# A diffusion block on one core: fewer VectorE instructions in the mixers and in the first norm

## The chip, the cores and the metric

The kernel runs on 1 core of one Trainium2 chip. The metric is the device time of one execution in microseconds (us); a lower one is better. Engines are named as in the profile: PE is TensorE's matmuls (PEld its weight loads), DVE is VectorE, ACT is ScalarE, POOL is GpSimd, and SP is SyncE, whose queue starts nearly all DMAs. Each engine works its own list of instructions strictly in order; a list is fixed when the kernel is built. Semaphores hold an instruction back until what it needs is done.

## The reference

One layer (DEPTH 1) on a latent stream of 1024 tokens and a context stream of 256, both 1024 wide. One input projection is split among four mixers (mLSTM in both directions, a spatial-gating MLP called SGU, a convolution module, a state-space scan S5 in both directions), their outputs are joined and projected, and two norms stand around a SwiGLU feed-forward network.

```python
h = x * (1.0 + sc1) + sh1
hc = xc * (1.0 + sc1c) + sh1c
z = h @ w_in_l
...
y_a, yc_a = mlstm_mixer(z[..., :OFF_B], zc_a, ...)        # two directions, summed, then normed per head
y_b = sgu_mixer(z[..., OFF_B:OFF_C], ...)                 # u * (w_s @ layer_norm(gelu(v)) + b_s)
y_c = conv_mixer(z[..., OFF_C:OFF_D], ...)                # silu(layer_norm(conv31(a * sigmoid(g))))
y_d, yc_d = s5_mixer(z[..., OFF_D:], zc_d, ...)           # complex scan, both directions
y = jnp.concatenate([y_a, y_b, y_c, y_d], axis=-1) @ w_out[l]
x = layer_norm(ALPHA * x + g1 * y, ln1_w[l], ln1_b[l])
x = layer_norm(ALPHA * x + g2 * swiglu(x * (1.0 + sc2) + sh2, w_ffn_in[l], w_ffn_out[l]), ln2_w[l], ln2_b[l])
```

## The kernel before, in words

Everything is fp32. A large product is made of three matmuls on parts: each operand is split into a high and a low part in a 32-bit matmul format (`split2`: ACT casts the high part, DVE subtracts to get the low one, lines L854 and L855), and PE adds hi*hi, hi*lo and lo*hi.

The program is written out mixer by mixer, and a scheduler at build time sorts the instructions into one list for each engine: it takes what it thinks ready, so that projections (`projT` L884, `projK` L893) fill PE between the small matmuls of the mixers. Tiles come from pools with a fixed number of buffers; a tile that takes over a buffer waits until the last reader of the tile before it is done.

The stages, by the time at which they run in the profile:

- up to 60 us: modulation, loads, splitting of the inputs.
- 60 to 220 us: S5. `s5_unit_tables` makes sine and cosine tables (`Es`, `Ec`) for four units; `s5_unit` projects two groups of states into PSUM (`X`, L287), turns them by the tables on DVE (`t1`, `t2`, `s`, L292 to L299), scans (L302), and turns them back (L306 to L310), for both directions `d`. For the reverse direction it reads `X` backwards in two pieces, since context (32 columns) and latent (128) are each reversed. `U`, the input in chunks, goes through DRAM (`zd`).
- 230 to 420 us: mLSTM in 8 chunks (`mlstm_chunk`; `mlstm_norm` for two chunks at a time), the convolution's taps on DVE, then SGU and the convolution's norm. `ln_stats` makes mean and 1/std with bn_stats on DVE and a square root on ACT; `sgu_norm` (L636) and `conv_norm` (L696) normalise on DVE.
- 375 to 496.5 us: `out_proj` for tokens 0 to 511 (half 0), interleaved with the mixers' end, then for half 1. For each of two column halves `c` and four token tiles `t` it adds 24 matmuls of 128x512 into a bank (L1184), DVE multiplies by the gate (L1188) and adds the residual into `XN` (L1189).
- `ln1(half)`: for each of four token tiles bn_stats on DVE (L1195), a square root on ACT (L1147), and on ACT the normalisation of 128x1024 (L1154); then for eight k four transposes on PE (L1204), two evacuations by ACT that apply the next modulation (`hi` L1207, `t_` L1208), and the low part on DVE (L1209). The results are the pages `H2`, which the feed-forward network reads. `page` gives buffers of a pool of 9, `page2` and `page3` those of two others.
- From 498.7 us: the feed-forward network (L884, then L1345 and L1470), and the second norm, which already makes its sums by accumulation (L1491, L1501).

Of the kernel before, what the change touches and what calls it, by code (L numbers as in the profile page):

```python
# [167 lines left out]
NP = 2  # L168


def s5_unit_tables(e, S, u, tp, wp):
# [77 lines left out]

    Ec, Es = (tp.tile([128, 2, NP, 160], F32, name=f"s5E{x}") for x in "cs")  # L250
    for d in range(2):
        f, n = Es[:, d], wp.tile([128, NP, 160], F32, name="s5ta", tag="s5ta")
# [13 lines left out]
        a.activation(Ec[:, d], Ec[:, d], AF.Copy, scale=-2.0, bias=1.0)  # L266
# [7 lines left out]
def s5_unit(e, S, T, u, U, Yg, wp):  # L274
# [4 lines left out]
    for P in range(NP):  # L279
        SS = []  # L280
        for d in range(2):
# [3 lines left out]
            for gi in range(2):  # L285
                for ri in range(2):
                    pe.matmul(X[gi * 64:(gi + 1) * 64, ri, :], lhsT=T.WT[:, P, d, ri, gi * 64:(gi + 1) * 64],  # L287
                              rhs=U(2 * (P0 + P) + gi), start=True, stop=True)
            t1, t2, s = (wp.tile([128, 2, 160], F32, name=f"s5{x}", tag=f"s5{x}") for x in ("r1", "r2", "sc"))
            Ec, Es = T.Ec[:, d, P, None, :], T.Es[:, d, P, None, :]  # L290
            if d == 0:
                v.tensor_tensor(t1, X, bc(Ec, [128, 2, 160]), op=MUL)  # L292
                v.tensor_tensor(t2, X, bc(Es, [128, 2, 160]), op=MUL)
            else:
                for t, E_ in ((t1, Ec), (t2, Es)):
                    v.tensor_tensor(t[:, :, 0:32], X[:, :, 31::-1], bc(E_[:, :, 0:32], [128, 2, 32]), op=MUL)
                    v.tensor_tensor(t[:, :, 32:160], X[:, :, 159:31:-1], bc(E_[:, :, 32:160], [128, 2, 128]), op=MUL)
            v.tensor_tensor(s[:, 0], t1[:, 0], t2[:, 1], op=ADD)
            v.tensor_tensor(s[:, 1], t1[:, 1], t2[:, 0], op=SUB)  # L299
            r8 = bc(S.r8[:, dp:dp + 1], [128, 160])  # L300
# [8 lines left out]
            v.tensor_tensor(o[:, 0], q1[:, 0], q2[:, 1], op=SUB)
            v.tensor_tensor(o[:, 1], q1[:, 1], q2[:, 0], op=ADD)  # L310
            SS.append(SD)
# [210 lines left out]
def mlstm_chunk(e, G, c, qT, kT, vx, hb, wp):  # L522
# [33 lines left out]
    for hh in range(2):  # L556
        for d in range(2):
            wi = G.TW[:, 1, d].rearrange("p (r h c) -> p r h c", r=2, h=2)
            v.tensor_tensor(tmp[:, d, hh * 2:hh * 2 + 2], I[hh][:, 0:260].rearrange("p (r d x) -> p r d x", r=2, d=2)[:, :, d],
                            bc(wi[:, :, hh, step(d):step(d) + 1], [128, 2, 65]), op=MUL)  # L560
    for d in range(2):
# [5 lines left out]
    for d in range(2):
        i = 2 + c if d == 0 else 9 - c
        dn = tmp[:, d, :, 64].rearrange("p (h r) -> p h r", h=2)
        g = G.TW[:, 2, d].rearrange("p (r h c) -> p h r c", r=2, h=2)[:, :, :, i]  # L570
        v.scalar_tensor_tensor(r[:, d], dn, -1.0, dn, op0=MUL, op1=MAX)
        v.tensor_tensor(r[:, d], r[:, d], g, op=MAX)
# [44 lines left out]
def ln_stats(e, srcs, wp, tag, n):  # L617
# [8 lines left out]
    e.nc.scalar.activation(mv[:, :, 1], mv[:, :, 1], AF.Sqrt)
# [57 lines left out]
def conv_norm(e, x, y, q, lnw, lnb, wp):  # L684
# [10 lines left out]
    for i in range(2):  # L695
        v.tensor_scalar(xn[:, i], ps[:, i * 256:(i + 1) * 256], mv[:, i, 0:1], mv[:, i, 1:2], op0=SUB, op1=MUL)  # L696
# [66 lines left out]
def body(tc, A, out):  # L763
# [5 lines left out]
    with st:  # L769
# [369 lines left out]

        lns = cp.tile([128, 8, 14], F32, name="Gk", tag="Gk")  # L1140

        def stats(t):

            st6, mv = lns[:, t, 0:12], lns[:, t, 12:14]
            v.bn_aggr(mv, st6)
            v.tensor_scalar(mv[:, 1:2], mv[:, 1:2], 1e-5, None, op0=ADD)
            a.activation(mv[:, 1:2], mv[:, 1:2], AF.Sqrt)  # L1147
            v.reciprocal(mv[:, 1:2], mv[:, 1:2])
            return mv

        def layer_norm(r, t, dst):
            mv = stats(t)
            v.tensor_scalar(mv[:, 0:1], mv[:, 0:1], mv[:, 1:2], -1.0, op0=MUL, op1=MUL)
            a.activation(dst, r, AF.Identity, scale=mv[:, 1:2], bias=mv[:, 0:1])  # L1154

# [8 lines left out]
        def out_proj(half):  # L1164
# [12 lines left out]
            for c in range(2):  # L1177
                cs_ = slice(c * 512, (c + 1) * 512)
                Ws = {kk: wtile(A["wo"][c, kk], 2, 512, pool_tag=tag) for kk, tag in ((3, None), (1, None), (2, page), (0, page))}
                for t in range(4):  # L1180
# [7 lines left out]
                    v.tensor_tensor(t_, ps, g1[:, cs_], op=MUL)  # L1188
                    v.scalar_tensor_tensor(x_, x_, ALPHA, t_, op0=MUL, op1=ADD)  # L1189

        def ln1(half, new):
            for t in range(half * 4, half * 4 + 4):
                xn = XN[t // 2][:, t % 2]
                for c in range(2):
                    v.bn_stats(lns[:, t, c * 6:c * 6 + 6], xn[:, c * 512:(c + 1) * 512])  # L1195
# [377 lines left out]
```

## Time and profile before

| | us |
|---|---|
| median of 3 runs (lowest to highest) | 1174.7 (1173.6 to 1176.86) |
| the profiled execution | 1174.02 |
| its span, first to last instruction | 1172.2 |
| PE busy | 1133.1 (97%) |
| DVE busy | 930.0 (79%) |
| ACT busy | 445.6 (38%) |

A row of the timeline gives the start, the duration, the engine, the line, the operation and its tiles, how many were merged (x), and in brackets the idle time before it with what ended it. A row of groups gives the count, then the busy time in us and the mean of one in ns, then the idle time before. A row of a window gives its length and each engine's busy time with its number of instructions, then PEclk, the share of the full clock that TensorE was granted. Matmuls are drawn longer than they hold the engine: twelve that start every 0.227 us are drawn at about 0.39 us each, so that PE looks busy through a wait of less than some 0.16 us.

### The profile page before, as it was taken

How to read it: one execution, taken by the hardware profiler on the slowest of the kernel's cores; microseconds unless marked ns; L12 is line 12 of the kernel's file. 1: busy time of each engine (PE TensorE's matmuls, PEld its weight loads, DVE VectorE, ACT ScalarE, POOL GpSimd, SP SyncE). 2: the span in 40 equal slices, each digit the busy share in tenths (PEclk: the TensorE clock that was granted, in tenths of full speed). 3: DMA queues.
4: the chain of work that ended last, by engine and by line, in shares of the span. 5: the costliest groups of instructions: out<-in, count | busy, mean ns of one | idle time of the engine just before them, and what ended most of it. 6: DMA issues, size and time to landing. Idle time of an engine off the chain costs nothing.

```text
span 1172.2 us, 15295 instructions
## 1 busy us (share of the span) xinstructions
PE 1133.1 (97%) x5671; PEld 895.4 (76%) x5671; DVE 930.0 (79%) x1851; ACT 445.6 (38%) x691; POOL 9.6 (1%) x30
## 2 busy tenths in 40 slices
PE   6999999999999999989999999999999999999996
PEld 1487788667888788868887888888887778888884
DVE  6588999978899889879968676777778767766775
ACT  1454444522326433582233332333232336433431
POOL 0010000000000000000000000000000000000000
PEclk9999999999999999999999999999999999999998
DMA  9542111022143346362333545345445679766621
GB/s 359 212 133 89 42 46 57 27 71 70 57 141 109 99 157 212 99 225 73 108 123 112 196 179 180 134 153 192 170 154 202 255 259 349 238 196 220 195 103 72
DMA packets 63147, 177.87 MB, mean 152 GB/s; under 512 B 5537, under 2 KB 9793, under 8 KB 61282
## 3 DMA queue, kind: packets, MB, share of 16 engines
q1 hardware_dynamic: 62658, 175.93, 43.3%
q8 instruction: 44, 0.72, 0.3%
q0 software_dynamic: 272, 0.70, 0.2%
q10 hardware_dynamic: 144, 0.29, 0.1%
q14 instruction: 29, 0.24, 0.1%
HBM read 136.54 MB, written 40.35 MB: 151 GB/s over the span
## 4 chain that ended last, share of the span: by engine, by line
PE 77%; DVE 13%; DMA 4%; issue 4%; ACT 2%; POOL 0%; DVEq 0%; ACTq 0%; POOLq 0%
PE mm L1345 16%; PE mm L884 13%; PE a L1345 8%; PE mm L1470 6%; PE mm L1184 4%; PE b L1345 4%; PE b L884 4%; PE a L1470 3%; PE b L1470 3%; PE mm L893 3%; PE c L1470 2%; PE b L564 1%; DVE whl L855 1%; DVE pg L855 1%; DMA raw<-in_w_dram 1%
## 5 line engine op out<-in xcount | busy, mean ns | idle before, releaser
L854 ACT CAST whl<-raw 128x512 fp32r<-128x512 f32 (+1 forms) x198 | 120.3, 622 | 283.2 <-PE mm L884 69.6
L884 PE MATMUL mm<-pg,whl 128*128 128x512 f32 x816 | 217.7, 406 | 1.4 <-ACT pg L1207 1.2
L1345 PE MATMUL mm<-pg,whl 128*128 128x512 f32 x864 | 205.9, 390 | 0.4 <-DVE whl L855 0.3
L1345 PEld LDWEIGHTS mm<-pg,whl 128*128 128x128 f32 x864 | 161.9, 188 | 35.6 <-issue 0.8
L884 PEld LDWEIGHTS mm<-pg,whl 128*128 128x128 f32 x816 | 147.7, 190 | 38.8 <-issue 6.1
L855 DVE TENSOR_TENSOR whl<-raw,whl 128x512 fp32r<-128x512 f32 (+1 forms) x198 | 133.6, 689 | 46.3 <-ACT whl L854 44.7
L1345 PE MATMUL a<-pg,whl 128*128 128x512 f32 x432 | 104.7, 390 | 3.6 <-ACT whl L854 3.6
L1345 PEld LDWEIGHTS a<-pg,whl 128*128 128x128 f32 x432 | 80.7, 188 | 21.3 <-ACT whl L854 4.8
L855 DVE TENSOR_TENSOR pg<-raw,pg 128x1024 fp32r<-128x1024 f32 (+1 forms) x52 | 59.6, 1149 | 20.8 <-ACT pg L854 20.7
L855 DVE TENSOR_TENSOR pg<-whl,pg 128x1024 fp32r<-128x1024 f32 (+1 forms) x42 | 47.4, 1133 | 31.9 <-ACT pg L854 31.6
L854 ACT CAST pg<-raw 128x1024 fp32r<-128x1024 f32 (+1 forms) x52 | 51.5, 992 | 48.9 <-DMA raw<-in_w_dram 18.0
L854 ACT CAST pg<-whl 128x1024 fp32r<-128x1024 f32 (+1 forms) x42 | 41.1, 980 | 65.9 <-PE c L1470 25.2
L893 PE MATMUL mm<-whl,pg 128*128 128x256 f32 (+1 forms) x448 | 63.1, 288 | 0.0
L893 PEld LDWEIGHTS mm<-whl,pg 128*128 128x128 f32 x448 | 58.1, 190 | 1.5 <-issue 1.1
L1345 PE MATMUL b<-pg,whl 128*128 128x512 f32 x216 | 51.9, 389 | 0.0
L1184 PE MATMUL mm<-pg 128*128 128x512 f32 x192 | 50.8, 409 | 0.0
L1184 PE MATMUL mm<-whl,pg 128*128 128x512 f32 x192 | 50.2, 398 | 0.3 <-DVE pg L1172 0.3
L1470 PE MATMUL mm<-pg,pg 128*128 128x512 f32 x171 | 48.0, 389 | 0.0
L1470 PE MATMUL a<-pg,pg 128*128 128x512 f32 x162 | 47.2, 390 | 0.2 <-DVE hs L1484 0.2
L1470 PE MATMUL b<-pg,pg 128*128 128x512 f32 x162 | 47.1, 389 | 0.0
L1345 PEld LDWEIGHTS b<-pg,whl 128*128 128x128 f32 x216 | 40.5, 188 | 8.4
L1184 PEld LDWEIGHTS mm<-pg 128*128 128x128 f32 x192 | 37.4, 198 | 8.6 <-DVE pg L855 0.7
(468 smaller groups left out, 1838.2 us busy)
## 6 DMA issues: line engine op xcount, KB each, us to landing
raw<-in_w_dram SPq DMA_DIRECT2D x59, 512.0 KB
gd<-pg SPq DMA_DIRECT2D x22, 1024.0 KB
whl<-gd SPq DMA_DIRECT2D x35, 512.0 KB
pg<-in_w2k_dram SPq DMA_DIRECT2D x11, 1024.0 KB
td<-pg SPq DMA_DIRECT2D x11, 1024.0 KB
raw<-td SPq DMA_DIRECT2D x20, 512.0 KB
pg<-in_wm_dram SPq DMA_DIRECT2D x16, 512.0 KB
raw<-in_wo_dram SPq DMA_DIRECT2D x16, 512.0 KB
```

The costliest lines, as they stand in the source:

```text
L564: pe.matmul(ps[:, x * 65:(x + 1) * 65], lhsT=D[d][:, x], rhs=vx[:, h, :], start=True, stop=True)
L854: a.copy(hi, r)
L855: v.tensor_tensor(lo, r, hi.bitcast(F32), op=SUB)
L884: pe.matmul(ps[h], lhsT=W(wi, k), rhs=rhs(hi, h, k), **f)
L893: pe.matmul(ps, lhsT=lhs(hi, k), rhs=Ws[k // 4](wi, k % 4), start=(k == 0 and n == 0), stop=(k == 7 and n == 2))
L1184: pe.matmul(ps, lhsT=Yr(hi, half, k)[:, t * 128:(t + 1) * 128], rhs=Ws[k // 2](wi, k % 2), start=(i + n == 0), stop=(i == 7 and n == 2))
L1345: pe.matmul(ps, lhsT=W[:, wi, k, :], rhs=B[b][hi][:, k], start=(first and k + n == 0), stop=(k == 3 and n == 2), skip_group_check=True)
L1470: pe.matmul(ps[t], lhsT=Ag[:, hi, k, t * 128:(t + 1) * 128], rhs=Bg[:, wi, k], start=(first and k0 + k + m == 0), stop=(k0 + k == NK - 1 a ...
```

## The change

Seven edits go together.

1. S5: the sine table `Es` holds both signs (`[-sin, sin]`, made by one more ACT copy), so that one instruction makes both parts of a rotated number; for the reverse direction the first 32 columns of `U` stand once more behind the latent ones (192 columns instead of 160, in DRAM and in SBUF), so that `X` is read backwards in one piece.
2. `BD` of the S5 tables moves from its own buffer to `cxn`, a buffer that the convolution's taps use later.
3. mLSTM: the weights `TW` of the reverse direction are turned into forward order when ACT makes them (six small instructions in place of one), and the chunk then works on both directions in one instruction.
4. `mlstm_norm` and `ln_stats` add epsilon as the bias of the square root; `ln_stats` also makes -mean/std.
5. `sgu_norm` and `conv_norm` normalise on ACT.
6. The first norm's sums come from the residual add in `out_proj` (accum_out); its squares come from a new ACT instruction over 128x1024 with an accumulator.
7. That instruction needs somewhere to write: `junk`, the first page of `H2` of the half. The pages of `H2` are therefore allocated before the norms.

```diff
     for d in range(2):
-        f, n = Es[:, d], wp.tile([128, NP, 160], F32, name="s5ta", tag="s5ta")
+        f, n = Es[:, d, :, 1], wp.tile([128, NP, 160], F32, name="s5ta", tag="s5ta")
...
         v.tensor_tensor(f, f, n, op=MUL)
+        a.activation(Es[:, d, :, 0], f, AF.Copy, scale=-1.0)
...
-            if d == 0:
-                v.tensor_tensor(t1, X, bc(Ec, [128, 2, 160]), op=MUL)
-                v.tensor_tensor(t2, X, bc(Es, [128, 2, 160]), op=MUL)
-            else:
-                for t, E_ in ((t1, Ec), (t2, Es)):
-                    v.tensor_tensor(t[:, :, 0:32], X[:, :, 31::-1], bc(E_[:, :, 0:32], [128, 2, 32]), op=MUL)
-                    v.tensor_tensor(t[:, :, 32:160], X[:, :, 159:31:-1], bc(E_[:, :, 32:160], [128, 2, 128]), op=MUL)
-            v.tensor_tensor(s[:, 0], t1[:, 0], t2[:, 1], op=ADD)
-            v.tensor_tensor(s[:, 1], t1[:, 1], t2[:, 0], op=SUB)
+            if d:
+                X = X[:, :, ::-1]
+            v.tensor_tensor(t1, X, bc(Ec, [128, 2, 160]), op=MUL)
+            v.tensor_tensor(t2, X, Es, op=MUL)
+            v.tensor_tensor(s, t1, t2[:, ::-1], op=ADD)
...
-            v.tensor_tensor(o[:, 0], q1[:, 0], q2[:, 1], op=SUB)
-            v.tensor_tensor(o[:, 1], q1[:, 1], q2[:, 0], op=ADD)
+            v.tensor_tensor(SD if d == 0 else SD[:, :, ::-1], q1, q2[:, ::-1], op=SUB)
...
-        for d in range(2):
-            wi = G.TW[:, 1, d].rearrange("p (r h c) -> p r h c", r=2, h=2)
-            v.tensor_tensor(tmp[:, d, hh * 2:hh * 2 + 2], I[hh][:, 0:260].rearrange("p (r d x) -> p r d x", r=2, d=2)[:, :, d],
-                            bc(wi[:, :, hh, step(d):step(d) + 1], [128, 2, 65]), op=MUL)
+        wi = G.TW[:, 1].rearrange("p d (r h c) -> p h r d c", r=2, h=2)
+        v.tensor_tensor(tmp.rearrange("p d (h r) x -> p h r d x", h=2)[:, hh], I[hh][:, 0:260].rearrange("p (r d x) -> p r d x", r=2, d=2),
+                        bc(wi[:, hh, :, :, 2 + c:3 + c], [128, 2, 2, 65]), op=MUL)
...
-        v.tensor_scalar(xn[:, i], ps[:, i * 256:(i + 1) * 256], mv[:, i, 0:1], mv[:, i, 1:2], op0=SUB, op1=MUL)
+        a.activation(xn[:, i], ps[:, i * 256:(i + 1) * 256], AF.Identity, scale=mv[:, i, 1:2], bias=mv[:, i, 0:1])
...
-            e.dma(zd[b], zs.rearrange("p s c -> p (s c)"))
-            Ub = s5.tile([128, 8, 160], F32, name="s5U", bufs=2)
+            e.dma(zd[b, :, :, 0:160], zs)
+            e.dma(zd[b, :, :, 160:192], zs[:, :, 0:32])
+            Ub = s5.tile([128, 8, 192], F32, name="s5U", bufs=2)
...
+        def layer_norm(r, t, junk):
+
+            s0, s1, mean, rstd, nb = (lns[:, t, i:i + 1] for i in range(5))
+            v.tensor_scalar(mean, s0, s1, -1.0 / D, op0=ADD, op1=MUL)
+            a.activation(junk, r, AF.Square, bias=mean, accum_out=rstd)
+            a.activation(rstd, rstd, AF.Sqrt, scale=1.0 / D, bias=e.eps)
+            v.reciprocal(rstd, rstd)
+            v.tensor_tensor(nb, mean, rstd, op=MUL)
+            a.activation(r, r, AF.Identity, scale=rstd, bias=nb)
...
-                    v.scalar_tensor_tensor(x_, x_, ALPHA, t_, op0=MUL, op1=ADD)
+                    v.scalar_tensor_tensor(x_, x_, ALPHA, t_, op0=MUL, op1=ADD, accum_out=lns[:, half * 4 + t, c:c + 1])
...
+            for kk in range(2):
+                for hl in range(2):
+                    H2[hl][half][kk] = new[kk]([128, 4, 512], F32R)
+            junk = H2[0][half][0].rearrange("p k t -> p (k t)")[:, 0:D]
             for t in range(half * 4, half * 4 + 4):
-                xn = XN[t // 2][:, t % 2]
-                for c in range(2):
-                    v.bn_stats(lns[:, t, c * 6:c * 6 + 6], xn[:, c * 512:(c + 1) * 512])
-                layer_norm(xn, t, xn)
+                layer_norm(XN[t // 2][:, t % 2], t, junk)
```

The scheduler sorts the changed program anew, and three places of its lists matter here. In the changed kernel the lines of `out_proj` are L1183, those of the first norm L1148 to L1153, the transposes L1201, the evacuations L1204 and L1205, `projT` L886.

ACT around the first norms, before: `pg_4059` and `pg_4061` are the rows `XN` of half 0, `pg2_4424` and `pg2_4426` those of half 1, and `pg_4736` is the first page of `H2`.

```order
L1154 ACTIVATE pg_4059<-pg_4059,Gk_3949 128x1024 [waits DVE_49]
L1154 ACTIVATE pg_4061<-pg_4061,Gk_3949 128x1024 [waits DVE_49]
L1147 ACTIVATE Gk_3949<-Gk_3949 128x1 [waits DVE_49] x2
L1154 ACTIVATE pg_4061<-pg_4061,Gk_3949 128x1024 [waits DVE_49]
L1154 ACTIVATE pg2_4424<-pg2_4424,Gk_3949 128x1024 [waits DVE_49]
L1147 ACTIVATE Gk_3949<-Gk_3949 128x1 [waits DVE_49]
L1154 ACTIVATE pg2_4424<-pg2_4424,Gk_3949 128x1024 [waits DVE_49]
```

The rows of half 0 come first, then those of half 1 as they get ready. Now, from the place at which half 0 begins (`pg_3991` and `pg_3993` are its rows, `pg2_4358` is the second pair of half 1, `pg_4636` is `junk`):

```order
L856 CAST whl_4897<-raw_4892 128x512 [waits PE_49]
L1149 ACTIVATE pg_4636,Gk_3881<-pg_3991,Gk_3881 128x1024 [waits PE_49]
L1150 ACTIVATE Gk_3881<-Gk_3881,oz_72 128x1 [waits Activation_49] x2
L1149 ACTIVATE pg_4636,Gk_3881<-pg_3991,Gk_3881 128x1024
L1150 ACTIVATE Gk_3881<-Gk_3881,oz_72 128x1 [waits Activation_49]
L1153 ACTIVATE pg_3991<-pg_3991,Gk_3881 128x1024 [waits DVE_49] x2
L1149 ACTIVATE pg_4636,Gk_3881<-pg_3993,Gk_3881 128x1024
L1153 ACTIVATE pg2_4358<-pg2_4358,Gk_3881 128x1024
L1150 ACTIVATE Gk_3881<-Gk_3881,oz_72 128x1 [waits Activation_49]
L1149 ACTIVATE pg_4636,Gk_3881<-pg_3993,Gk_3881 128x1024
L1153 ACTIVATE pg_3993<-pg_3993,Gk_3881 128x1024 [waits DVE_49]
L1150 ACTIVATE Gk_3881<-Gk_3881,oz_72 128x1 [waits Activation_49]
```

Half 0's norms moved behind three of half 1's four squares, and the first of them waits for PE: `pg_4636` lies in the buffer that `pg_4345`, a low part of `out_proj(1)`'s input, held, and the matmul waited for is that page's last reader. After the rows shown come the fourth square of half 1, the last normalisation of half 0, a square root, and then the first evacuation.

PE at the end of `out_proj(1)`, before:

```order
L1184 MATMUL mm_4676<-pg_4589,pg_4419 128x512
L1184 MATMUL mm_4676<-pg_4589,pg_4418 128x512
L1204 MATMUL a_4738<-cst_71,pg_4059 128x128 [waits DMAHW2_49,Activation_49]
L1204 MATMUL a_4738<-cst_71,pg_4059 128x128 [waits Activation_49]
L1204 MATMUL a_4738<-cst_71,pg_4061 128x128 [waits DMAHW3_49,Activation_49]
L1204 MATMUL a_4738<-cst_71,pg_4061 128x128 [waits Activation_49]
L1204 MATMUL b_4747<-cst_71,pg_4059 128x128 x2
```

And now, from the last reader of `pg_4345`, the first row:

```order
L1183 MATMUL mm_4608<-pg_4516,pg_4345 128x512
L1183 MATMUL mm_4608<-pg_4516,pg_4344 128x512
L1183 MATMUL mm_4608<-pg_4521,pg_4350 128x512
L1183 MATMUL mm_4608<-pg_4521,pg_4351 128x512
L1183 MATMUL mm_4608<-pg_4521,pg_4350 128x512 x2
L1183 MATMUL mm_4608<-pg_4521,pg_4351 128x512
L1183 MATMUL mm_4608<-pg_4521,pg_4350 128x512
L1201 MATMUL a_4664<-cst_71,pg_3991 128x128 [waits DMAHW4_49,Activation_49]
L1201 MATMUL b_4673<-cst_71,pg_3991 128x128
L1201 MATMUL a_4682<-cst_71,pg_3991 128x128
```

Seven matmuls of `out_proj` stand behind that reader. The 16 transposes that follow went tile by tile of k before (four token tiles for one k) and go token tile by token tile now; in both lists the first matmul of the feed-forward network stands behind all 16 and behind the first evacuation.

PE at the last chunk of mLSTM (`c` = 7), whose last products are `L564` before (`L568` now), before:

```order
L691 MATMUL c<-cst,ap 64x128 x8
L1184 MATMUL mm<-pg 128x512
L564 MATMUL b<-vx,mD 128x65 x4
L554 MATMUL a<-mC,pg_2539 128x130 x4
L564 MATMUL b<-vx,mD 128x65 x4
L1184 MATMUL mm<-pg 128x512 x29
```

And now:

```order
L691 MATMUL c<-cst,ap 64x128 x5
L1183 MATMUL mm<-pg 128x512 x11
L568 MATMUL b<-vx,mD 128x65 x2
L1183 MATMUL mm<-pg 128x512 x2
L568 MATMUL b<-vx,mD 128x65 x2
L1183 MATMUL mm<-pg 128x512
```

Eleven matmuls of `out_proj(0)` moved ahead of the product instead of one. Over PE's whole list up to the end of `out_proj(1)` the boundaries between runs of large matmuls (projections and `out_proj`) and small ones are 257 before and 289 now.

More of the change, by code (lines that the diff above doesn't have):

```diff
@@ L217, in s5_unit_tables @@
                                -1.0, t2.rearrange("n P l q -> n (P l q)"), op0=MUL, op1=SUB)
-    BD = wp.tile([128, 4, NP, 32], F32, name="s5BD", tag="s5BD")
+    BD = e.mx.tile([128, 4, NP, 32], F32, name="cxn", tag="cxn")
     nc.gpsimd.memset(BD, 0.0)
@@ L248, in s5_unit_tables @@
             e.dma(M[:, P, gi, :], bass.AP(tensor=dr.tensor, offset=dr.offset + o, ap=[[16, 8], [NP * 240, 16], [1, 128]]))
-    Ec, Es = (tp.tile([128, 2, NP, 160], F32, name=f"s5E{x}") for x in "cs")
+    Ec = tp.tile([128, 2, NP, 160], F32, name="s5Ec")
+    Es = tp.tile([128, 2, NP, 2, 160], F32, name="s5Es")
     for d in range(2):
-        f, n = Es[:, d], wp.tile([128, NP, 160], F32, name="s5ta", tag="s5ta")
+        f, n = Es[:, d, :, 1], wp.tile([128, NP, 160], F32, name="s5ta", tag="s5ta")
         for P in range(NP):
@@ L470, in mlstm_gates @@
     for d in range(2):
-        a.activation(G.TW[:, :, d], ps[:, 0:3 * N].rearrange("p (i n) -> p i n", i=3)[:, :, d * 64:d * 64 + 40], AF.Exp)
+        pv = ps[:, 0:3 * N].rearrange("p (i n) -> p i n", i=3)[:, :, d * 64:d * 64 + 40]
+        if d == 0:
+            a.activation(G.TW[:, :, d], pv, AF.Exp)
+        else:
+            pv, tv = (x.rearrange("p i (h c) -> p i h c", h=4) for x in (pv, G.TW[:, :, d]))
+            for i in range(3):
+                a.activation(tv[:, i, :, 1::-1], pv[:, i, :, 0:2], AF.Exp)
+                a.activation(tv[:, i, :, 9:1:-1], pv[:, i, :, 2:10], AF.Exp)
     return G
@@ L481, in delta @@
     def delta(ps, d, i, k, vv):
+        if d:
+            i = 1 - i if i < 2 else 11 - i
         ke = wp.tile([128, 4, 64], F32, name="mke", tag="mtmp", bufs=2)
@@ L566, in mlstm_chunk @@
     r = wp.tile([128, 2, 2, 2], F32, name="mr")
[L567 to L572, printed above, removed]
+    dn = tmp[:, :, :, 64].rearrange("p d (h r) -> p d h r", h=2)
+    v.scalar_tensor_tensor(r, dn, -1.0, dn, op0=MUL, op1=MAX)
+    v.tensor_tensor(r, r, G.TW[:, 2].rearrange("p d (r h c) -> p d h r c", r=2, h=2)[:, :, :, :, 2 + c], op=MAX)
     rf = r.rearrange("p d h r -> p (d h r)")
@@ L592, in mlstm_norm @@
     v.tensor_reduce(mu, sq, axis=mybir.AxisListType.X, op=ADD)
-    v.tensor_scalar(mu, mu, 1.0 / 64, 1e-5, op0=MUL, op1=ADD)
-    a.activation(mu, mu, AF.Sqrt)
+    a.activation(mu, mu, AF.Sqrt, scale=1.0 / 64, bias=e.eps)
     v.reciprocal(mu, mu)
@@ L635, in sgu_norm @@
         g = gv[:, c0 + i]
-        e.nc.vector.tensor_scalar(g, g, mv[:, i, 0:1], mv[:, i, 1:2], op0=SUB, op1=MUL)
+        e.nc.scalar.activation(g, g, AF.Identity, scale=mv[:, i, 1:2], bias=mv[:, i, 0:1])
 def sgu_mix(e, vn, h, wsT, B, lnw, yT, wp):
@@ L796, in body @@
         e.ident, e.jrow, e.dl16, e.dl4, e.rst = (cst[:, off[n]] for n in ("ident", "jrow", "dl16", "dl4", "rst"))
-        oz = cp.tile([128, 2], F32, name="oz")
+        oz = cp.tile([128, 3], F32, name="oz")
         v.memset(oz[:, 0:1], 1.0)
         v.memset(oz[:, 1:2], 0.0)
-        e.one, e.zero = oz[:, 0:1], oz[:, 1:2]
+        v.memset(oz[:, 2:3], 1e-5)
+        e.one, e.zero, e.eps = (oz[:, i:i + 1] for i in range(3))
         ccol = cp.tile([128, 16], F32, name="ccol")
@@ L1138, in body @@
         s2, b2 = (cp.tile([128, 8], F32, name=n) for n in ("s2", "b2"))
[L1140 to L1154, printed above, removed]
+        lns = cp.tile([128, 8, 5], F32, name="Gk", tag="Gk")
+        def layer_norm(r, t, junk):
[6 more added lines that the diff above has]
+            a.activation(r, r, AF.Identity, scale=rstd, bias=nb)
         XN = []
```

19 lines of the change are left out of this document (8 added, 11 removed).

## The prediction

> **What bounds the kernel now.** I read the busy shares first, then the windows by stage, then PE's waits, then the timeline at the two places where the lists of the changed kernel differ most.
>
> ```profile
> PE 1133.1 (97%) x5671; PEld 895.4 (76%) x5671; DVE 930.0 (79%) x1851; ACT 445.6 (38%) x691; POOL 9.6 (1%) x30
> ```
>
> ```profile
> 60.00:496.50 436.50, 429.44 (x2621) 340.91 (x2621) 394.34 (x1016) 181.69 (x308) 7.45 (x13) 0.99 0.29 93
> 496.50:530.00 33.50, 29.97 (x154) 22.61 (x153) 26.81 (x36) 28.89 (x41) 0.00 (x0) 1.00 0.59 216
> 530.00:1172.00 642.00, 624.11 (x2737) 512.46 (x2735) 470.86 (x660) 215.41 (x312) 0.00 (x0) 0.99 0.50 176
> ```
>
> PE is the engine to watch in all three stages. In the mixers with `out_proj` (first row) it is busy 429.4 of 436.5 us while DVE is busy 394.3. From 530 us on it is PE alone, and nothing there changes: 0. The middle row, first norm and start of the feed-forward network, is the only one in which ACT comes near PE (28.9 against 30.0 of 33.5 us), and the change gives ACT four squares per half there. PE's waits in the first stage, the longest and the shortest of the ten listed:
>
> ```profile
> PE b L564 <- DVE mD L548: 1.6, 1, 1.6
> PE b L431 <- ACT mC L424: 0.9, 1, 0.9
> ...
> PE b L600 <- DVE msq L596: 0.3, 1, 0.3
> ```
>
> The ten add up to 6.9 us. That is all the waiting that the profile shows there, whatever DVE saves. Waits under some 0.16 us are hidden, since matmuls are drawn longer than they hold PE.
>
> **The first norm: ACT gets a queue at the wrong moment.** At the end of `out_proj(1)` (PE, then ACT by the timeline, then groups):
>
> ```profile
> 493.78 2.89 PE L1184 MATMUL mm<-pg 128*128 128x512 f32 x12
> 496.51 0.60 PE L1204 MATMUL a<-cst,pg 128*128 128x128 f32 x4
> ...
> 498.72 0.49 PE L884 MATMUL mm<-pg,whl 128*128 128x512 f32 x1 [0.30 <-ACT pg L1207]
> ```
>
> ```profile
> 478.37 1.24 ACT L1154 ACTIVATE pg<-pg,Gk 128x1024 f32<-128x1024 f32 x1
> ...
> 488.12 1.25 ACT L1154 ACTIVATE pg<-pg,Gk 128x1024 f32<-128x1024 f32 x1 [0.20 <-DVE Gk L1153]
> 489.27 0.18 ACT L1147 ACTIVATE Gk<-Gk 128x1 f32<-128x1 f32 x1
> ...
> 497.91 0.76 ACT L1207 ACTIVATE pg<-a,b,s 128x512 fp32r<-128x512 f32 x1
> ```
>
> ```profile
> L1501 ACT ACTIVATE pg<-pg,Gk 128x1024 f32<-128x1024 f32 x8 | 9.2, 1147 | 33.8 <-DVE Gk L1500 33.8
> L1501 ACT ACTIVATION_READ_ACCUMULATOR pg<-pg,Gk 128x1 f32 x8 | 1.5, 184 | 0.0
> L1147 ACT ACTIVATE Gk<-Gk 128x1 f32<-128x1 f32 x8 | 1.6, 204 | 9.4 <-DVE Gk L1146 9.4
> L1195 DVE BATCH_NORM_STATS2 Gk<-pg 128x6 f32<-128x512 f32 x16 | 10.6, 670 | 0.0
> ```
>
> Before, half 0's normalisations run from 478 us on, under 18 us of `out_proj(1)`; PE goes from its last matmul over 16 transposes to the first feed-forward matmul in 498.72 − 496.51 = 2.2 us. Call the end of `out_proj(1)` T. In the changed lists, half 0's squares write `junk`, in the buffer that the low part of `out_proj(1)`'s input held. Its last reader has seven matmuls behind it, 7 × 0.227 = 1.6 us (the twelve from 493.78 hold PE until 496.51, 0.227 each). So the first square can go no sooner than T − 1.6; ACT has a cast of some 0.6 us ahead and one semaphore to pass, so I start it at T − 0.8. Queued behind it on ACT, before the first evacuation: five squares (half 0's four, half 1's fourth), five normalisations, six roots. The same square with its accumulator read stands in the second norm: 1.147 + 0.184 = 1.33. So 5 × 1.33 + 5 × 1.245 (row 488.12) + 6 × 0.204 = 14.1 us; consecutive ones overlap by 0.1 (488.12 + 1.25 is 489.37, the next starts at 489.27), 0.8 over the lot, so 13.3; two round trips through DVE for the reciprocal, 0.5 (one waits 0.20 at 488.12); the evacuation 0.8. The first feed-forward matmul starts at T − 0.8 + 13.3 + 0.5 + 0.8 = T + 13.8 instead of T + 2.2: **+11.6** (ends +10.6 and +12.6, by the overlaps). Nothing covers it: PE's list has only the 16 transposes there. Of the 3.5 us that PE already idles in 496.5 to 530, I take back 1.5, since weights and evacuations come early then (ends 0 and −3.5).
>
> DVE loses the 16 bn_stats there, 10.6 us, and this is worth 0: DVE isn't on that path, ACT is. What DVE saves turns into waiting for ACT's squares.
>
> **The clock after a wait.** Two stretches in the mixers show a granted clock of half, one behind the longest wait of all:
>
> ```profile
> 406.70:413.50 6.80, 6.80 (x20) 5.73 (x21) 3.33 (x15) 0.72 (x2) 0.00 (x0) 0.50 0.87 283
> 239.50:242.80 3.30, 3.30 (x9) 2.62 (x9) 3.17 (x13) 0.00 (x0) 0.00 (x0) 0.50 0.00 0
> ```
>
> ```profile
> 396.89 0.48 PE L1184 MATMUL mm<-pg 128*128 128x512 f32 x1
> 397.30 0.72 PE L554 MATMUL a<-mC,pg 64*128 64x130 f32 x8
> ...
> 404.59 1.33 PE L564 MATMUL b<-vx,mD 128*128 128x65 f32 x8 [1.56 <-DVE mD L548]
> ```
>
> A spell of 3.3 to 6.8 us at half clock costs half of its length, 1.7 to 3.4. A wait of 11 us by the norm should bring such a spell: **+2.5**, the middle; ends 0 (the transposes may count as work) and +3.4. The Trainium skill, "TensorE: Matmul & The Clock Gate", section "Part 1: The HAM clock gate (the "warmup" mystery)", says that the clock is halved after at least one idle window of about 3.4 us and full again after about as long of sustained work. That rule speaks against this change, since the new wait is over three such windows; by it the term would be an estimated +1.7. The trace differs in both directions: 1.56 us of waiting stand ahead of the spell here, and it lasts 6.8 us.
>
> The other way round, the spell at 406.7 may vanish, because eleven `out_proj` matmuls instead of one now stand ahead of the `L564` that waits 1.56 us: 10 × 0.227 = 2.3 us of work covers it. I take **−3.4** (ends 0 and −5.1, if the spell at 239.5 goes too).
>
> **DVE in the mixers.** What it saves:
>
> ```profile
> L292 DVE TENSOR_TENSOR s5r<-b,s5Ec 128x320 f32<-128x320 f32 x8 | 3.8, 481 | 0.0
> L296 DVE TENSOR_TENSOR s5r<-b,s5Ec 128x64 f32<-128x64 f32 x8 | 1.7, 216 | 0.0
> L297 DVE TENSOR_TENSOR s5r<-b,s5Ec 128x256 f32<-128x256 f32 x8 | 3.3, 412 | 0.0
> L298 DVE TENSOR_TENSOR s5sc<-s5r,s5r 128x160 f32<-128x160 f32 x16 | 5.1, 317 | 0.0
> L309 DVE TENSOR_TENSOR s5S<-s5r,s5sc 128x128 f32<-128x128 f32 x16 | 4.5, 283 | 0.0
> L559 DVE TENSOR_TENSOR mtmp<-a,mTW 128x130 f32<-128x130 f32 x32 | 7.4, 284 | 6.0 <-PE a L554 6.0
> L565 DVE TENSOR_TENSOR mtmp<-mtmp,b 128x260 f32<-128x260 f32 x16 | 6.2, 416 | 0.4 <-PE b L564 0.4
> L696 DVE TENSOR_SCALAR cxn<-c,cmv 128x256 f32<-128x256 f32 x8 | 4.0, 538 | 0.0
> ```
>
> S5: two sums of 0.317 become one of 0.481, 16 times, −2.4; two of 0.283 become one of 256 elements (0.412), 16 times, −2.5; in the reverse direction two of 0.216 and two of 0.412 become two of 0.481, 8 times, −2.4. Together −7.3. mLSTM: four of 0.284 become two of 260 elements (0.416), 8 chunks, −2.4, and as much again for four small ones per chunk that become two. The 16 normalisations that go to ACT, at most 16 × 0.538 = −8.6. Together about −20 us of DVE's 394.3. PE was the bound, so this pays only where PE waits. Of the 6.9 us shown I take −3: part of them end on ACT, and a list sorted anew makes waits of its own (ends 0 and −6.9). Of the hidden ones I take **−2**; ends 0 and 20 − 6.9 = −13, if every microsecond of DVE had been on the path.
>
> What PE pays: there are 32 more boundaries between large and small matmuls, that is 16 more insertions. The single L1184 at 396.89 holds PE 397.30 − 396.89 = 0.41 where one of a run holds it 0.227: 16 × 0.18 = **+2.9**, ends 0 and +2.9 (in a run already broken it costs nothing).
>
> **At no cost, with their cover.**
>
> ```profile
> L266 ACT ACTIVATE s5Ec<-s5Ec 128x320 f32<-128x320 f32 x8 | 3.6, 455 | 0.0
> L626 ACT ACT_TABLE_LOAD x4 | 5.1, 1283 | 0.1
> L287 PE MATMUL b<-s5U,s5W x32: 299/299/350, 76.9 to 85.8; 128*64 128x160 f32 x32
> L785 SPq DMA_DIRECT2D s5U<-zd x16: 577/577/729, 70.0 to 87.2; - x16
> ```
>
> ACT in the mixers gains eight copies of the sine (8 × 0.455), 16 normalisations, five more small exponentials and four table loads (4 × 1.283), some 17 us on 181.7 of 436.5: it is idle more than half of the time, so 0. If that cover fails at the table loads alone, +5.1. The wider `U` puts one more DMA ahead of the loads of each part on SP's queue; the loads issue from 70.0 and the first reader is at 76.9, so 0, and at the far end two transfers of the size of those loads' issue, 2 × 0.6 = +1.2. `BD` in `cxn` puts a wait ahead of taps that DVE can do later: 0 (between 0 and +1). Epsilon as a bias takes away one small DVE instruction per norm, which is in the 20.
>
> **Sum.** +11.6 − 1.5 + 2.5 for the norm, −3.4 − 3 − 2 + 2.9 for the mixers: 12.6 − 5.5 = +7.1. Against the profiled execution, 1174.02 (span 1172.2 and 1.8 around it), this gives 1181.1. The median of the runs is 1174.7, 0.7 above that execution, so against it I say 1182.
>
> **The rivals.**
>
> *DVE was the bound in the mixers* (faster). For it: DVE is busy 90% there, and hidden waits can't be read. Against it: only 6.9 us of waits are shown, and part end on ACT. Then the mixers give 6.9 + 5.1 + up to 13 = 25 against 14.1 − 1.5 at the norm; halfway into the hidden waits the mixers give back 18, PE's boundaries take none, and with 12.6 off that the time is near 1169; at the far end 1162. It decides from the point at which the mixers give over 16 us.
>
> *Even*: the mixers give 9 to 16, the norm takes 12.6, and it ends within 3.5 us of before, 0.3%, about what a measurement of this kernel can tell from no change: near 1175.
>
> *Nothing given back* (slower still): the list sorted anew waits on the four table loads and keeps its clock spells, 0 to +5.1 from the mixers, with +12.6 to +14.5 at the norm: 1187 to 1194.
>
> *The norm's wait doesn't come*: it would need ACT to get at half 0 earlier, which its order forbids, as every engine works strictly in order. It has no chance of its own.
>
> **How the numbers follow.** My forecast (+3.5 to +12.3, its own range 1178 to 1187) 0.58; nothing given back 0.14; even 0.16; faster 0.12. So slower 0.72, same 0.16, faster 0.12. The range 1172 to 1191 leaves out nearly all of the faster case, a little of the worst and of the even one, 0.2 together.
>
> **What would show it.** In the profile of the changed kernel: ACT's first squares of half 0 waiting for PE, and starting within 2 us of `out_proj(1)`'s end; PE idle some 11 us there, its first feed-forward matmul released by ACT's evacuation; a granted clock under 1 in the 10 us behind. `out_proj(1)` should end near 491 us (496.5 − 5.5), the `L564` of the last chunk without its wait, and full clock after it. I am wrong if the squares run under `out_proj(1)` (then about 1169), if `out_proj(1)` ends at 480 or before (DVE was the bound), or behind 497 (then the mixers pay too).

## The result and the profile after

The changed kernel took 1185.4 us (median of 4 runs, 1183.0 to 1186.15) against 1175.65 for the kernel before beside it: ratio 1.0081, 95% interval [1.0059, 1.0104]. The forecast was 1182, slower. The profiled execution took 1186.09, its span 1184.3, which is 12.1 us over the span of before; the medians differ by 9.75. Where a time from a trace follows, it is this execution's.

The busy shares of the changed kernel, then its windows (to the end of `out_proj(1)`, at 498.9 us; the start of the feed-forward network; the rest; then two stretches at half clock):

```profile
PE 1137.9 (96%) x5671; PEld 899.1 (76%) x5671; DVE 909.6 (77%) x1744; ACT 471.7 (40%) x740; POOL 9.9 (1%) x30
```

```profile
60.00:498.90 438.90, 429.90 (x2622) 340.32 (x2620) 374.65 (x900) 197.53 (x339) 7.79 (x13) 1.00 0.29 94
498.90:530.00 31.10, 22.48 (x107) 16.57 (x107) 19.00 (x35) 30.22 (x48) 0.00 (x0) 0.78 0.61 215
530.00:1184.30 654.30, 636.28 (x2785) 523.00 (x2783) 477.96 (x669) 224.45 (x326) 0.00 (x0) 0.99 0.50 174
457.60:461.00 3.40, 3.40 (x10) 2.64 (x9) 3.40 (x5) 0.00 (x0) 0.00 (x0) 0.50 0.62 199
502.00:515.70 13.70, 8.39 (x27) 5.77 (x28) 3.33 (x9) 13.32 (x21) 0.00 (x0) 0.50 0.22 68
```

DVE is down by 19.7 us in the first stage (394.34 to 374.65), and the stage is no shorter. In the second PE is busy 22.5 of 31.1 us and ACT 30.2: ACT has become the bound there. PE's timeline at that place, then ACT's:

```profile
496.19 2.88 PE L1183 MATMUL mm<-pg 128*128 128x512 f32 x12
502.14 0.48 PE L1201 MATMUL a<-cst,pg 128*128 128x128 f32 x1 [3.07 <-ACT pg L1153]
...
507.99 0.48 PE L1201 MATMUL a<-cst,pg 128*128 128x128 f32 x1 [3.60 <-ACT pg L1153]
...
510.43 0.48 PE L1201 MATMUL a<-cst,pg 128*128 128x128 f32 x1 [1.33 <-ACT pg L1153]
...
511.78 0.79 PE L886 MATMUL mm<-pg,whl 128*128 128x512 f32 x1 [0.23 <-ACT pg L1204]
```

```profile
497.38 0.60 ACT L856 CAST whl<-raw 128x512 fp32r<-128x512 f32 x1
497.89 1.15 ACT L1149 ACTIVATE pg<-pg,Gk 128x1024 fp32r<-128x1024 f32 x1
...
509.16 1.22 ACT L1153 ACTIVATE pg<-pg,Gk 128x1024 f32<-128x1024 f32 x1
510.29 0.28 ACT L1150 ACTIVATE Gk<-Gk,oz 128x1 f32<-128x1 f32 x1
510.95 0.78 ACT L1204 ACTIVATE pg<-a,b,s 128x512 fp32r<-128x512 f32 x1 [0.38 <-PE a L1201]
```

Twelve matmuls from 496.19 hold PE until 498.91. Half 0's first square starts 1.0 us before that, and ACT then works through squares, roots and normalisations without a break of more than 0.15 us until the last root at 510.29; the first evacuation stands at 510.95. No idle time of ACT that ends on PE stands ahead of that first square: it follows the cast before it at once. What holds it there is its place in ACT's list, and the first experiment below shows what gave it that place. The first feed-forward matmul comes 511.78 − 498.91 = 12.87 us after `out_proj(1)`, against 2.21 before. PE's waits in the mixers, the longest and the shortest of twelve that add up to 8.2 us:

```profile
PE mm L886 <- ACT whl L856: 1.7, 1, 1.7
PE mm L1183 <- DVE pg L1171: 1.4, 1, 1.4
...
PE mm L895 <- DVE Gk L959: 0.2, 1, 0.2
```

The wait of the last mLSTM chunk's product (1.6 us) is gone, and two that weren't there stand at the head.

### The profile page after: what moved, and what is told of

Its sections match the earlier page's. It is cut to its first block, busy times and chain, and to the rows that moved or that the text cites. A ratio compares the mean times of both kernels' runs of the same rounds, so it can differ in the third digit from the quotient of the medians.

```text
span 1184.3 us, 15233 instructions
## 1 busy us (share of the span) xinstructions
PE 1137.9 (96%) x5671; PEld 899.1 (76%) x5671; DVE 909.6 (77%) x1744; ACT 471.7 (40%) x740; POOL 9.9 (1%) x30
## 4 chain that ended last, share of the span: by engine, by line
PE 77%; DVE 13%; ACT 4%; DMA 3%; issue 2%; POOL 0%; DVEq 0%; ACTq 0%; POOLq 0%
PE mm L1342 16%; PE mm L886 13%; PE a L1342 8%; PE mm L1467 5%; PE mm L1183 5%; PE b L1342 4%; PE b L886 4%; PE mm L895 4%; PE a L1467 3%; PE b L1467 3%; PE c L1467 2%; DVE pg L857 2%; DVE whl L857 1%; PE b L568 1%; DVE pg L1503 1%
## 5 line engine op out<-in xcount | busy, mean ns | idle before, releaser
L886 PE MATMUL mm<-pg,whl 128*128 128x512 f32 x816 | 216.6, 405 | 1.9 <-ACT whl L856 1.7
L886 PEld LDWEIGHTS mm<-pg,whl 128*128 128x128 f32 x816 | 147.2, 189 | 38.9 <-issue 5.9
L1183 PE MATMUL mm<-pg 128*128 128x512 f32 x192 | 50.9, 406 | 0.5 <-DVE pg L857 0.5
L1183 PE MATMUL mm<-whl,pg 128*128 128x512 f32 x192 | 49.4, 396 | 1.4 <-DVE pg L1171 1.4
L1183 PEld LDWEIGHTS mm<-pg 128*128 128x128 f32 x192 | 36.2, 193 | 9.4 <-DVE pg L857 1.8
```

Of the source, the lines that this page charges most:

```text
L886: pe.matmul(ps[h], lhsT=W(wi, k), rhs=rhs(hi, h, k), **f)
L1183: pe.matmul(ps, lhsT=Yr(hi, half, k)[:, t * 128:(t + 1) * 128], rhs=Ws[k // 2](wi, k % 2), start=(i + n == 0), stop=(i == 7 and n == 2))
```

## Experiments

Theory A is the prediction's: the norm costs what it does because its squares write into a buffer that `out_proj(1)` still reads. Its rival B says that eight more ACT instructions of 1.3 us are the cost wherever they write; C, that the mixers pay. D and E are about what DVE saves: under D each microsecond of DVE in the mixers is on the path and the change lost its gain elsewhere, under E DVE had just enough room, so that less of it wins little.

**The same kernel with another page for `junk`.**

```diff
-            junk = H2[0][half][0].rearrange("p k t -> p (k t)")[:, 0:D]
+            junk = H2[0][half][1].rearrange("p k t -> p (k t)")[:, 0:D]
```

> The changed kernel with one index changed: junk is the third page of H2 of the half instead of the first; for half 0 that page comes from another pool. Theory A (the wait for the buffer that out_proj(1) reads is the cost): half 0's four squares run during out_proj(1), the gap from its last matmul to the first feed-forward matmul falls from 12.9 us to 2 to 4, no half clock behind it, and the time from 1185.4 to about 1175 (1173 to 1178). Theory B (eight more ACT instructions of 1.3 us are the cost, wherever they write): the gap stays over 8 us and the time within 3 us of 1185.

Measured: 1174.77 us, ratio 1.0006 [0.9990, 1.0022]. The wait is gone; PE's timeline, then two rows of ACT's, the fourth square of half 0 and the third of half 1:

```profile
495.19 2.89 PE L1183 MATMUL mm<-pg 128*128 128x512 f32 x12
497.91 0.60 PE L1201 MATMUL a<-cst,pg 128*128 128x128 f32 x4
...
499.97 0.50 PE L886 MATMUL mm<-pg,whl 128*128 128x512 f32 x1
```

```profile
474.43 1.15 ACT L1149 ACTIVATE pg<-pg,Gk 128x1024 fp32r<-128x1024 f32 x1
...
495.23 1.15 ACT L1149 ACTIVATE pg<-pg,Gk 128x1024 fp32r<-128x1024 f32 x1
```

With one index changed, half 0's squares have another place in ACT's list; they are done over 20 us before `out_proj(1)` ends, and three of half 1's ahead of its end too; the gap from 497.91 to 499.97 is 2.06 us. B falls, since the same eight squares are still there, and 10.6 us of the median hang on one index (1185.4 − 1174.8).

**Each side alone.** Three kernels: edits 1 to 5 with the old norm; edits 6 and 7 on the kernel before; the same with `junk` in the third page.

```diff
 # mixers_only: the changed kernel, but
-                layer_norm(XN[t // 2][:, t % 2], t, junk)
+                for c in range(2):
+                    v.bn_stats(lns[:, t, c * 6:c * 6 + 6], xn[:, c * 512:(c + 1) * 512])
+                layer_norm(xn, t, xn)
...
 # norm_only: the kernel before, but
...
+            junk = H2[0][half][0].rearrange("p k t -> p (k t)")[:, 0:D]
...
 # norm_only_p2: the kernel before, but
...
+            junk = H2[0][half][1].rearrange("p k t -> p (k t)")[:, 0:D]
```

> The changed kernel with the first norm as before (edits 1 to 5 alone). Theory A: out_proj(1) ends about 2.4 us later than in the kernel before, as in the changed kernel (498.9 against 496.5), the gap to the first feed-forward matmul is 2 to 3 us, time 1175 to 1178. If DVE's 20 us in the mixers are worth something and only the norm's new order spoiled it: out_proj(1) ends at 490 or before, time about 1169. If the mixers are what costs (theory C): over 1180.

> The kernel before with edits 6 and 7 alone (sums by accumulation, squares on ACT, junk in the first page of H2). Its ACT list has the same order as the changed kernel's: half 0's squares behind three of half 1's, waiting for PE. Theory A and B: gap of 12 to 14 us, clock at half behind it, time about 1183 (1181 to 1186). Theory C (the mixers are what costs): within 3 us of the kernel before, 1175.

> As norm_only, with junk in the third page of H2. Theory A: the gap is 2 to 4 us, time as before, 1175 (1172 to 1177), since the 10.6 us of DVE's bn_stats were hidden. Theory B: about 1183.

Measured: 1177.15 (ratio 1.0020 [1.0006, 1.0035]), 1188.3 (1.0121 [1.0098, 1.0143]) and 1177.51 (1.0019 [1.0002, 1.0036]). The gaps are 2.21, 12.87 and 2.06 us. The wait is there with the old mixers too, to the hundredth, and costs 10.8 us between the last two. C falls as the main cause: the mixers' edits alone cost some 2 us. Two forecasts were missed by time: `norm_only` is above its range by 2.3, `norm_only_p2` by 0.5. In both, `out_proj(1)` ends later than before (502.1 and 500.6 against 496.5) though no mixer was touched; why isn't settled, and the profiled execution of `norm_only` is the slowest of its six.

That the norm's 10.6 us of bn_stats are worth nothing stands in the third kernel, that what the mixers save on DVE is worth nothing in the first. This saving is smaller than it was taken for. The first stage of `mixers_only`:

```profile
60.00:498.20 438.20, 430.37 (x2628) 341.57 (x2628) 384.96 (x918) 196.59 (x341) 7.58 (x13) 1.00 0.30 94
```

DVE is busy 384.96 us there against 394.34 before: 9.4 us less. The rest of the changed kernel's 19.7 is left for edits 6 and 7: 15 of the 16 bn_stats ran ahead of the end of `out_proj(1)` before.

**Is DVE on the path? More of it instead of less.** On the kernel before, and on the one without the norm's wait:

```diff
 # dve_more: the kernel before, L298, L299 and L559 done twice
+            for _ in range(2):
+                v.tensor_tensor(s[:, 0], t1[:, 0], t2[:, 1], op=ADD)
+                v.tensor_tensor(s[:, 1], t1[:, 1], t2[:, 0], op=SUB)
...
 # p2_dve_more: junk_page2, the same two steps done twice
+            for _ in range(2):
+                v.tensor_tensor(s, t1, t2[:, ::-1], op=ADD)
...
```

> The kernel before with DVE work added instead of removed: the two sums of S5's rotation (L298, L299) and the four products of an mLSTM chunk (L559) are each done twice, 32 x 0.317 + 32 x 0.284 = 19.2 us more on DVE in the mixers, as much as the change takes away there. Theory A (PE's list is the bound in the mixers and DVE has slack): out_proj(1) ends within 4 us of 496.5, time 1175 to 1179. Theory D (DVE was on the path and the change's saving was lost to something else in the new order): out_proj(1) ends 10 to 19 us later, time 1185 to 1194.

> junk_page2 (the changed kernel without the norm's wait) with the sum of S5's rotation and mLSTM's product each done twice: 16 x 0.48 + 16 x 0.42 = 14.4 us more on DVE in the mixers, which still leaves DVE some 6 us under the kernel before. Theory E (the change's saving is slack: DVE was just below the point at which PE has to wait, so that more costs all of it and less wins little): 1174 to 1178, out_proj(1) ends within 3 us of 498. Theory D (any microsecond of DVE in the mixers is on the path): 1187 to 1190.

Measured: 1198.49 (ratio 1.0210 [1.0185, 1.0235]), 24 us more than before; and 1177.53 (1.0035 [1.0017, 1.0053]), 2.8 us more than `junk_page2`. The 19 and 14 us of the forecasts are sums of drawn durations, and these overlap. Two adds of S5 in a row, in the kernel before, are drawn at 0.33 and 0.32 us but start 0.24 us apart:

```profile
80.29 0.33 DVE L298 TENSOR_TENSOR s5sc<-s5r,s5r 128x160 f32<-128x160 f32 x1
80.53 0.32 DVE L299 TENSOR_TENSOR s5sc<-s5r,s5r 128x160 f32<-128x160 f32 x1
80.76 0.86 DVE L302 TENSOR_TENSOR_SCAN s5r<-s5r,s5sc 128x160 f32<-128x160 f32 x2
```

DVE's busy time to the end of `out_proj(1)` says how much was added: 11.5 us in `dve_more` (394.34 to 405.85, its row stands below) and 11.4 in `p2_dve_more` (374.19 to 385.61; `junk_page2`, then `p2_dve_more`):

```profile
60.00:497.90 437.90, 429.28 (x2619) 339.88 (x2618) 374.19 (x909) 206.41 (x355) 7.93 (x13) 1.00 0.30 95
60.00:497.10 437.10, 426.01 (x2621) 337.51 (x2620) 385.61 (x941) 210.61 (x358) 7.82 (x13) 1.00 0.30 95
```

Neither D nor A alone fits: 11.5 us more on the kernel before cost twice that, 11.4 us more on `junk_page2` cost 2.8, and the 19.7 us less of the change won nothing. What the 24 us are, by `dve_more`'s waits and windows (to the end of its `out_proj(1)`, and one of its stretches at half clock):

```profile
PE mm L1186 <- DVE pg L1174: 5.4, 3, 2.8
PE b L202 <- DVE s5S L193: 2.8, 1, 2.8
PE b L566 <- DVE mD L549: 1.8, 1, 1.8
...
```

```profile
60.00:520.50 460.50, 444.90 (x2618) 350.35 (x2617) 405.85 (x1079) 187.74 (x312) 7.99 (x13) 0.96 0.28 88
381.80:395.50 13.70, 13.36 (x58) 10.42 (x60) 9.65 (x37) 3.05 (x5) 0.00 (x0) 0.50 0.11 45
```

The waits grow from 6.7 to 15.0 us, and the clock is at half in 34 us instead of 10. In `p2_dve_more` DVE is busy 385.6 us, still under the 394.3 of before, and most of the addition is hidden: the change had bought slack. That is what E forecast. One rival isn't separated from it: the lists of both kernels were sorted anew as well (large and small matmuls meet at 297 places in `dve_more`, at 291 before), so that part of the 24 us may come from the order.

**The three parts of the mixers alone**, each on the kernel before: edits 1 and 2; edit 3; edits 4 and 5. The lines are those of the change, so no diff is shown again.

> The kernel before with edits 1 and 2 alone (S5, BD in cxn): DVE about 7 us less between 60 and 220 us, two more DMAs, eight ACT copies. Theory A: within 3 us of 1175. Theory D: 1168 to 1171. If the wider U or BD's new buffer costs: S5's last product later than 220.5 by 2 or more and the time 1177 to 1179.

> The kernel before with edit 3 alone (both directions at once in mLSTM): DVE about 5 us less between 270 and 410 us. Theory A: within 3 us of 1175. Theory D: about 1170. If waiting for both directions' data costs, a new wait at L559's or L565's place and 1177 to 1179.

> The kernel before with edits 4 and 5 alone (normalisation on ACT, epsilon as a bias): DVE 8 us less, ACT 8 us and some table loads more. Theory A: within 3 us of 1175. Theory D: 1167 to 1170. If the trip to ACT costs: a wait of PE for ACT at the transposes L647 or L700 and 1177 to 1180.

Measured: 1176.25 (ratio 1.0018 [1.0000, 1.0036]), 1170.64 (0.9964 [0.9949, 0.9980]), 1174.83 (1.0002 [0.9986, 1.0018]). In the first stage the S5 edit takes 3.4 us of busy time from DVE (394.3 to 390.9) and wins nothing, the normalisation on ACT 3.7 (to 390.6) and wins nothing. The mLSTM edit takes 3.7 too (to 390.6), and it is a real gain of some 4 us, more than A allowed it and what D forecast for it. Three savings of one size with such different results don't fit D, and the amount saved isn't what decides. PE at the last chunk in `s5_only`, then in `mlstm_only`:

```profile
403.17 0.51 PE L1182 MATMUL mm<-pg 128*128 128x512 f32 x1
405.24 1.33 PE L560 MATMUL b<-vx,mD 128*128 128x65 f32 x8 [1.56 <-DVE mD L544]
```

```profile
403.36 1.20 PE L1189 MATMUL mm<-pg 128*128 128x512 f32 x4
404.39 0.56 PE L572 MATMUL b<-vx,mD 128*128 128x65 f32 x4
404.75 0.71 PE L1189 MATMUL mm<-pg 128*128 128x512 f32 x2
```

With the S5 edit the wait of 1.56 us stands as before, and a spell at half clock follows it from 406.6 on. With the mLSTM edit `out_proj` matmuls come in between, the wait is gone, and no spell at half clock is left between 60 us and the end of `out_proj(1)`, which ends at 490.1 instead of 496.5. The lost wait alone doesn't make the gain: in `actnorm_only` it is gone as well, but spells at half clock came at 351.3 and 450.3, beside waits of 0.9 and 2.0 us.

The stage is best read as a sum. From each profiled execution: the end T of `out_proj(1)`; PE's waits of over 0.15 us between 60 us and T; half the length of the stretches at half clock there; and the rest, T − 60 less these two.

| | T | waits | clock | rest |
|---|---|---|---|---|
| before | 496.5 | 6.7 | 5.1 | 424.7 |
| `dve_more` | 520.5 | 15.0 | 17.1 | 428.4 |
| `s5_only` | 496.7 | 7.5 | 3.4 | 425.8 |
| `mlstm_only` | 490.1 | 5.0 | 0.0 | 425.1 |
| `actnorm_only` | 500.8 | 7.9 | 6.8 | 426.1 |
| `p2_dve_more` | 497.1 | 10.4 | 0.0 | 426.7 |
| `junk_page2` | 497.9 | 7.7 | 1.7 | 428.5 |
| `mixers_only` | 498.2 | 7.2 | 1.7 | 429.3 |
| changed | 498.9 | 8.2 | 1.7 | 429.0 |

The rest moves by less than 5 us, whatever DVE does: it is mostly PE's own list, with whatever waits are too short to show. What less work on DVE can win is mainly the 12 us of waits and clock of the kernel before; what more of it can cost has no such end. How much of the 12 us is had goes with the order that the lists come out in, and the mixers' edits together, in `mixers_only`, `junk_page2` and the changed kernel, have 2 to 4 us more of the rest than each part alone. Against the kernel before these lie in stalls of under 0.3 us at many places, most between 300 and 330 and between 390 and 420 us; what makes them isn't settled.

Each row is one execution, and executions of one kernel differ by their spells: the twelve of `p2_dve_more` reach from 1173.39 us at a mean clock of 0.995, the one in the table, to 1181.61 at 0.988, and 0.007 of the clock is 8.2 us of such a span, as much as lies between the two times. The row of `mlstm_only` is also the fastest of its twelve (1166.57 against a median of 1170.64), so part of its 490.1 is luck. The mean over all executions is safer. Span times the share of the clock that was not granted is 12.5 us in the kernel before and 9.4 in `mlstm_only`, which is 3.1 of the 3.9 us between their mean times: its gain is mostly clock. For `junk_page2` the same figure falls by 2.8 (12.7 to 9.9) and the rest of its span grows by 3.1, so that the changed mixers do win some clock and lose it again in the rest.

**Is the half clock behind the norm's wait a price of its own?** 72 transposes that nobody reads keep PE at work in the wait; they read the last `t_` of `out_proj(1)`.

```diff
+            if warm is not None:
+                ps = e.ps("c")
+                for j in range(72):
+                    pe.transpose(ps[:, j % 4 * 128:j % 4 * 128 + 128], warm[:, 0:128], e.ident)
```

> The changed kernel with 72 transposes of a row block that nobody reads put on PE between out_proj(1) and the first norm's transposes: about 8 us of work inside the 10.7 us in which PE waits. ACT's order is unchanged, so the gap to the first feed-forward matmul stays 12 to 13 us. If the half clock behind the wait has a price of its own (theory A: it ran from 502.0 to 515.7 us, and 3.9 us of feed-forward matmuls lie in it, 1.9 us lost): no spell behind the first norm, the stretch from the first feed-forward matmul to its second stage 2 us shorter, time about 1183.5. If the clock falls anyway, or the price lies in the gap alone: 1185 to 1186.

Measured: 1184.93 (ratio 1.0101 [1.0076, 1.0126]), not to be told from the changed kernel by time. The trace tells more (a window, then PE's timeline):

```profile
502.00:515.70 13.70, 11.14 (x80) 8.84 (x78) 4.22 (x10) 13.46 (x21) 0.00 (x0) 1.00 0.19 60
```

```profile
499.10 8.08 PE L1195 MATMUL c<-cst,hs 128*128 128x128 f32 x72 [0.79 <-DVE hs L1187]
...
510.88 0.50 PE L886 MATMUL mm<-pg,whl 128*128 128x512 f32 x1 [0.54 <-ACT pg L1209]
...
608.18 1.07 PE L1346 MATMUL mm<-pg,whl 128*128 128x512 f32 x4
```

The next stage of the changed kernel begins here:

```profile
609.09 1.30 PE L1342 MATMUL mm<-pg,whl 128*128 128x512 f32 x5
```

The clock stays full, the gap is 12.73 us. But from the first feed-forward matmul to the first one of the next stage it is 608.2 − 510.9 = 97.3 us, and in the changed kernel, with its clock at half, 609.1 − 511.8 = 97.3 too. The stretch is not 2 us shorter, as a price of the spell would have it: the spell costs nothing that shows there.

**A version that beats both.** The mLSTM edit and the norm with `junk` in the third page:

> The kernel before with the mLSTM edit and the norm's sums by accumulation with junk in the third page (edits 3, 6 and 7). The mLSTM edit alone gave 0.9964, the norm so placed 1.0019. If the gain of the mLSTM edit is its lost wait at the last chunk and the clock spell behind it, it stays: 1170 to 1173, no half clock near 406 us. If it hangs on one lucky order: 1174 to 1178.

Measured: 1170.16 us, ratio 0.9962 [0.9945, 0.9979]; `out_proj(1)` ends at 493.8, the gap is 2.06, and there is no half clock near 406 us. It and the mLSTM edit alone (1170.64) are the best of all; between the two nothing can be told.

## Why the prediction came out as it did

The direction, the place and the size of the main term were right. That the sum came within 4 us of the median is in part luck: the norm was put 4.7 us too high and the mixers 7.9 too low.

- *The norm's wait, +11.6.* Right: 12.87 − 2.21 = +10.7. The square began at T − 1.0 (forecast T − 0.8) behind the cast named, and the chain from there to the evacuation took 13.1 us (forecast 13.8). That 16 bn_stats less are worth nothing held as well. The sign that these squares wait for PE came only in part: the first one starts 0.6 us after the point T − 1.6 that its last reader set, but ACT, busy with what stands ahead, shows no wait for PE.
- *The clock behind it, +2.5.* Wrong: 0. The spell came and lasted 13.7 us, twice as long as the longest row of before. What failed is the step "a spell costs half of its length". Over whole executions, in which PE is the bound, that step fits (the 8.2 us of `p2_dve_more` above); here ACT, busy 30.2 of 31.1 us, was the bound. The Trainium skill, "TensorE: Matmul & The Clock Gate", section "Part 1: The HAM clock gate (the "warmup" mystery)", says that the clock is halved after an idle window of about 3.4 us. The trace agrees on the onset (502.0, 3.1 us after PE's last `out_proj` matmul, with 3.07 us of idle time shown there), but in the mixers spells follow waits of 1.4 and 1.56 us, well under such a window. The spells of 3.4, 6.8, 10.2 and 13.7 us that these runs show between 60 and 1000 us are once, twice, three and four times that length; the estimate of +1.7 by that page isn't borne out.
- *What is taken back, −1.5.* −2.8 (from the first feed-forward matmul to the next stage 100.1 us before, 97.3 after), inside its ends.
- *PE's waits in the mixers, −3, and the hidden ones, −2.* Wrong in sign: the waits went from 6.7 to 8.2. The longest one went, and two of its size came, for an ACT cast (`L886`) and for DVE's low part (`L1183`). The saving behind this term was mis-sized as well: "about −20 us" adds up drawn durations, which overlap, and the busy time of DVE fell by 9.4 in `mixers_only`.
- *The spell at 406.7 gone, −3.4.* Right, and the one at 239.4 went too, but a new one of 3.4 us came at 457.6, one microsecond behind the wait of 1.4 us at `L1183`: 5.1 − 1.7 = −3.4.
- *32 more boundaries, +2.9.* Wrong by a miscount, which also stands in the section on the change: lines of the two kernels were mixed up. With the same lines counted in both there are 291 boundaries before and 289 now, so this term should have been 0. The rest of the stage grew by 4.3 us all the same, for another reason, unsettled (above).

In all +10.7 − 2.8 + 0 at the norm, 7.9 where 12.6 was forecast; and +2.4 in the mixers (T 496.5 to 498.9) where −5.5 was. T behind 497 is one of the prediction's own signs of being wrong, and `mixers_only` bears it out: the mixers pay too. Norm and mixers make +10.3 at the second stage of the feed-forward network (598.8 to 609.1). The other 1.8 us of this execution come later: a stretch of 6.8 us at half clock from 959.4 on, which begins inside a wait of 2.9 us, where the execution before waited 2.5 and kept its clock. The difference of the medians, 9.75, is about the first part alone.

Of the rivals, the one on the other side ("DVE was the bound") was half right in a way that the prediction didn't have: more work on DVE did cost time, in `dve_more`, but less of it won none, in the changed mixers.

## What to carry to other kernels

Before a scratch output is put into a buffer that "is free anyway", ask who read it last and when that reader is done: here one index, a page of another pool, is worth 10.6 us. And before a nearly full engine is relieved, add up the waits and the clock losses of the engine that bounds the stage: little more than that can be won (12 us here), while an addition to the same engine may cost more than itself. What is saved or added is read from busy time, since drawn durations overlap.

## What was not expected of the hardware

The cost of an engine at its edge was lopsided: 11.5 us more of DVE's busy time came with 24 us more, 8 of them shown as PE's waits and 12 as half clock, while 19.7 us less gave nothing; how much of the 24 is the new order of the lists isn't shown. And a clock at half for 13.7 us cost nothing measurable where ACT was the bound: here the granted clock of a stretch had no price where PE wasn't what the stretch waited for.
